# Moving the convolution statistics of a conformer/mLSTM block: none in the first head, the first mean product behind the second head's key projection

## The chip, the cores and the metric

The kernel runs on one core of one Trainium2 chip. The metric is the device time of one execution in microseconds (us); the time of a kernel is the median of several executions. A profile is taken of one execution more, and its times are counted from the start of its span. The engines are PE (TensorE, matrix products), DVE (VectorE), ACT (ScalarE), POOL (GpSimd) and SP, which here only issues DMAs. Each takes its own instructions in a fixed order that is set when the kernel is built; waits on semaphores tie the engines together.

## What is computed

One layer of a hybrid backbone over 512 latent tokens (a 1024-wide model) with 256 context tokens. Cut to the parts that matter here:

```
h  = adaLN(RMSNorm(x))                                  # latent and context tokens
p  = split(h @ w_in)                                    # GLU pair, q, k, v, output gate, scan gates, branch gates
u  = p[0] * sigmoid(p[1])                               # GLU, 1024 channels
u  = depthwise_conv(u, width 31, along rows of 64 tokens)
A  = silu(layernorm(u, over the 1024 channels)) @ w_conv_out     # branch A
B  = (norm(mLSTM(q, k, v)) * sigmoid(p[5])) @ w_m_out            # branch B, 4 heads, both directions
x += gate1 * ((sigmoid(p[7]) * A + sigmoid(p[8]) * B) @ w_out)
x += gate2 * squared_relu_mlp(adaLN(RMSNorm(x)))
out = RMSNorm(x)
```

The layer norm of branch A needs, for each token, the mean and the mean square over all 1024 channels.

## The kernel before, in words

All matrix products with weights are done in three passes: each operand is split into a high and a low half (`split`, `wpiece`), and `mm3` (lines 105 to 108) issues high x high, high x low and low x high. `mlast[0]` holds the last matmul that `mm3` issued. A weight piece of 512 KB is loaded by SP into `wraw` (three buffers), its high half made by ACT (line 100) and its low half by DVE (line 101), four buffers of each.

The stages run in this order: modulation and the six early branch-gate tiles; more gate tiles and the queries of head 0 (`q_proj`); the scan gates; the keys of head 0 (`k_proj`); then the loop over four heads (lines 653 to 665); then the tail with branch A's and B's output products and the MLP.

For heads 1 to 3 the loop runs `k_proj(h)`, in heads 1 and 3 one `glu_tile`, `q_proj(h)` and `attend`; `attend` also does the two steps of another GLU tile among the scores (heads 0 to 2), and a further `glu_tile` follows it (heads 0 to 2). So the eight GLU tiles of 128 channels are spread as two in head 0, three in head 1, two in head 2 and one in head 3.

`attend` computes the head's output gate (`p5`), for four query tiles of 128 tokens the scores (`spc`, `spl`) and the weights `pm_`, transposes those on PE (`tp`), then the six value tiles (`pv`, 144 matmuls), and then the output of the four query tiles (`po`). The value tiles take two PSUM banks of the one tag and four of the other; the tag "b" has four banks and serves `tp`, the GLU products `pg`, the queries `pq`, four of the value tiles, `po`, and the mean product `pm0`.

A GLU tile ends in `conv31`: 31 taps on a tile of 128 channels x 512 tokens. The first is ACT's (line 431), the other 30 are DVE's (line 433), one instruction each, into an accumulator `ca` (two buffers) from the padded input `up` (two buffers). The taps are given a priority lowered by 800, so that the scheduler, which fixes the order of each engine's instructions before the run, uses them to fill in among others. `conv31` then puts one portion, `lnstat(j, ...)`, into the list `queue`; `pump(n)` takes up to n portions from that list and issues them where it is called.

`lnstat` (lines 443 to 456) is what the change moves. For tile 0 it first makes a rough mean per token: a product of the matrix of ones with the convolved tile into `pm0` (line 446; an fp32 product, which the trace shows as two matmuls on a tile it calls `pm`), and ACT's copy of it into `lnm0` (line 447). Every tile then has this mean subtracted (DVE, line 448) and is stored to DRAM (SP, line 449); its sum and its squares are collected in two running tiles, by ACT for tile 0 (lines 451, 452) and by ACT and DVE for the others (454 to 456). `lnfinish` (lines 458 to 469) turns the two into the mean and the reciprocal deviation in the last head.

Before the change `pump(9)` is called in every head at two places in `attend`: ahead of the value projection (line 586) and behind the outputs (line 630). In the last head `lnend` calls it once more ahead of `lnfinish`. Since the list is never longer than nine, each call empties it. The calls ahead of the value projection therefore issue tile 0 in head 0; tiles 1, 2 and 3 in head 1; tiles 4 and 5 in head 2; tiles 6 and 7 in head 3; the calls behind the outputs find nothing.

Of the kernel before, what the change touches and what calls it, by code (L numbers as in the profile page):

```python
# [47 lines left out]
def block(ctx, tc, a, out):  # L48
    nc = tc.nc
    mm = nc.tensor.matmul  # L50
# [11 lines left out]
    ones = cst.tile([P, P], F32, name="ones")  # L62
# [26 lines left out]
    mlast = [None]  # L89
# [51 lines left out]
    def pump(n):  # L141
        while n > 0 and queue:
            queue.popleft()()
            n -= 1

    with ExitStack() as hs:
# [9 lines left out]
        def bank(nm):  # L156
            return ps.tile([P, 512], F32, tag="b", name=nm, bufs=4)
# [211 lines left out]
        def qk_tile(h, i, which, hi, lo):  # L369
            f = (16 if which == "k" else 0) + 4 * h + i  # L370
            w = wpiece(a["wqk"][f], (KT, P))
            raw = hq2.tile([P, 774], F32, tag="craw", name="craw")
            acc = hq2.tile([P, 770], F32, tag="cacc", name="cacc")
            wc = O_QK + 5 * f
            if which == "k":
                pk, pl = bank_a("pk"), bank_a("pl")
                projT(pk, w, 0, C)
                projT(pl, w, C, T)
                for o in (0, 258, 772):
                    nc.gpsimd.memset(raw[:, o:o + 2], 0.0)  # L380
                nc.scalar.copy(out=raw[:, 2:258], in_=pk[:, 0:C])
                nc.scalar.copy(out=raw[:, 260:772], in_=pl)
                n, segs = 770, ((0, 0, C), (258, C, T))
            else:
                pk = bank("pq")
                projT(pk, w, C, T)
                for o in (0, 514):
                    nc.gpsimd.memset(raw[:, o:o + 2], 0.0)
                nc.scalar.copy(out=raw[:, 2:514], in_=pk)
                n, segs = 512, ((0, 0, T),)  # L390
            nc.scalar.activation(out=acc[:, :n], in_=raw[:, 0:n], func=AF.Copy, scale=ccol(wc))  # L391
            for d in range(1, 5):
                nc.vector.scalar_tensor_tensor(out=acc[:, :n], in0=raw[:, d:d + n], scalar=ccol(wc + d),  # L393
                                               in1=acc[:, :n], op0=ALU.mult, op1=ALU.add)
            tot = segs[-1][1] + segs[-1][2]
            for s, o, m in segs:
                nc.scalar.activation(out=raw[:, o:o + m], in_=acc[:, s:s + m], func=AF.Silu)
            split(hi[:, i, :], lo[:, i, :], raw[:, :tot])
            tick()

        def glu_steps(j):
            up = hq2.tile([P, 8, 94], F32, tag="up", name="up")
            u = up[:, :, 15:79]

            def step(s):
                w = wpiece(a["wglu"][s, j], (KT, P))
                pg = bank("pg")
                projT(pg, w, C, T)
                pv = pg.rearrange("p (r c) -> p r c", r=8)
                if s:  # L410
                    nc.gpsimd.memset(up[:, :, 0:15], 0.0)
                    nc.gpsimd.memset(up[:, :, 79:94], 0.0)
                    nc.scalar.activation(out=u, in_=pv, func=AF.Sigmoid)
                else:
                    nc.vector.tensor_tensor(out=u, in0=pv, in1=u, op=ALU.mult)
                    conv31(j, up)
                tick()
            return [lambda: step(1), lambda: step(0)]

        def glu_tile(j):  # L420
            for st in glu_steps(j):
                st()

        def conv31(j, up):
            acc = hqa.tile([P, T], F32, tag="ca", name="ca", bufs=2)
            accv = acc.rearrange("p (r c) -> p r c", r=8)

            def tap(d):
                w_ = ccol(O_DW + 31 * j + d)
                if d == 0:  # L430
                    nc.scalar.activation(out=accv, in_=up[:, :, 0:64], func=AF.Copy, scale=w_)
                else:
                    nc.vector.scalar_tensor_tensor(out=accv, in0=up[:, :, d:d + 64], scalar=w_, in1=accv,  # L433
                                                   op0=ALU.mult, op1=ALU.add)
            with tc.high_priority(offset=-LOWP):
                for d in range(31):
                    tap(d)
            queue.append(lambda: lnstat(j, acc, up.rearrange("p r c -> p (r c)")[:, :T]))
# [4 lines left out]
        def lnstat(j, acc, sq):  # L443
            if j == 0:
                pm0 = bank("pm0")
                mm(pm0, lhsT=ones, rhs=acc, start=True, stop=True)
                nc.scalar.activation(out=ln["m0"], in_=pm0, func=AF.Copy, scale=1.0 / P)
            nc.vector.tensor_tensor(out=acc, in0=acc, in1=ln["m0"], op=ALU.subtract)
            nc.sync.dma_start(out=cdr[j], in_=acc)
            if j == 0:  # L450
                nc.scalar.copy(out=ln["s1"], in_=acc)
                nc.scalar.activation(out=ln["s2"], in_=acc, func=AF.Square)
            else:
                nc.scalar.activation(out=sq, in_=acc, func=AF.Square)
                nc.vector.tensor_tensor(out=ln["s1"], in0=ln["s1"], in1=acc, op=ALU.add)
                nc.vector.tensor_tensor(out=ln["s2"], in0=ln["s2"], in1=sq, op=ALU.add)
# [14 lines left out]
        def ab_early(i):  # L471
            w = wpiece(a["wab"][i - NS], (KT, P))
            pg = bank("pab")
            projT(pg, w, C, T)
            so = hq2.tile([P, T], F32, tag="cacc", name="so")
            nc.scalar.activation(out=so, in_=pg, func=AF.Sigmoid)
            nc.sync.dma_start(out=sd[i], in_=so)
            tick()

        def k_proj(h):  # L480
            khi = pools["kv"].tile([P, 4, TOK], F32R, tag="kvh", name="khi")
            klo = pools["kv"].tile([P, 4, TOK], F32R, tag="kvl", name="klo")
            for i in range(4):
                qk_tile(h, i, "k", khi, klo)
            return khi, klo

        def q_proj(h):
            qhi = hq.tile([P, 4, T], F32R, tag="qh", name="qhi")
            qlo = hq.tile([P, 4, T], F32R, tag="ql", name="qlo")
            for i in range(4):  # L490
                qk_tile(h, i, "q", qhi, qlo)
            return qhi, qlo
# [14 lines left out]
        def attend(h, he, he2, khi, klo, qhi, qlo, more, mid):  # L507
# [15 lines left out]
            for t in range(NT):  # L523
# [59 lines left out]
                    js = slice(3 * hf, 3 * hf + 3)  # L583
                    split(pth[:, js, :], ptl[:, js, :], tp[:, :384].rearrange("p (j t) -> p j t", j=3))
                Ps.append((pth, ptl))
            pump(9)
            nc.scalar.activation(out=sg, in_=sg, func=AF.Sigmoid)
            vhi = pools["kv"].tile([P, 6, HD], F32R, tag="kvh", name="vhi")
            vlo = pools["kv"].tile([P, 6, HD], F32R, tag="kvl", name="vlo")
# [23 lines left out]
            for t in range(NT):  # L613
# [13 lines left out]
                pend = (t, hm)  # L627
                if mid and t == 1:
                    mid()
            pump(9)  # L630
            if h == H - 1:
                store(*pend)

# [19 lines left out]
        for h in range(H):  # L653
            if h:
                kh = k_proj(h)
                if h == 1 or h == H - 1:
                    glu_tile(next(glus))
                qh = q_proj(h)
            if h < H - 1:
                attend(h, he, he2, *kh, *qh, lambda: glu_steps(next(glus)), None)  # L660
            else:
                attend(h, he, he2, *kh, *qh,
                              lambda: [lambda i=i: ab_early(i) for i in range(NS + NX, NS + NX + NE)], lnend)
            if h < H - 1:
                glu_tile(next(glus))
# [403 lines left out]
def build(shapes):  # L1069
    import concourse.bacc as bacc  # L1070
    import concourse.tile as tile

    nc = bacc.Bacc("TRN2", target_bir_lowering=False, num_devices=1, dynamic_dma_scratch_size=4096)
    aps = {k: nc.dram_tensor(f"in_{k}", s, F32, kind="ExternalInput").ap() for k, s in shapes.items()}
    out = nc.dram_tensor("out_0_dram", (T, D), F32, kind="ExternalOutput").ap()
    with tile.TileContext(nc) as tc:
        block(tc, aps, out)
    return nc
# [10 lines left out]
```

## Time and profile before

| | us |
|---|---|
| median of 3 runs | 1362.58 |
| lowest and highest of them | 1361.43, 1363.29 |
| the profiled execution, its own time | 1359.83 |
| its span, from the first to the last instruction | 1358.1 |
| busy PE, weight loads of PE, DVE, ACT, POOL | 1316.8, 1096.3, 949.6, 591.3, 63.3 |
| mean granted clock of PE, share of full | 0.991 |

A row of a group or a timeline gives the line of the kernel, the engine and operation, the written tile `<-` the read tiles, and the shapes; "x18" is the number of instructions merged into the row. In square brackets stands the idle time of the engine ahead of it and what ended that. Matmuls are pipelined, so the step from one start to the next is their cost and not the duration shown. Heads are found in the trace by their tiles: head 0's value matmuls begin at 208.12 us, head 1's at 406.56, head 2's at 573.56, head 3's at 751.44.

### The profile page before, as it was taken

The numbers are of one execution on the slowest core, as the hardware profiler recorded it, in microseconds if no ns is written. First come the engines' busy times: TensorE is split into PE (matmuls) and PEld (weight loads), VectorE is DVE, ScalarE is ACT, GpSimd is POOL, SyncE is SP. The second block draws the span as 40 slices with busy tenths as digits, with TensorE's granted clock in tenths as the row PEclk, the third lists the DMA queues.
The fourth block names the chain that finished last, engine by engine and source line by source line (L and its number), as shares of the span: only waits on it lengthen the run. The fifth ranks groups of instructions, "written<-read, shape, count | busy, mean of one in ns | idle before, by whom it ended". The sixth has DMA issues, their size and how long they took to land. (4 is left out here: it accounts for less than half of the span.)

```text
span 1358.1 us, 16564 instructions
## 1 busy us (share of the span) xinstructions
PE 1316.8 (97%) x6214; PEld 1096.3 (81%) x6214; DVE 949.6 (70%) x1480; ACT 591.3 (44%) x857; POOL 63.3 (5%) x223
## 2 busy tenths in 40 slices
PE   6999995999999999999999999999999999999997
PEld 4778883888888888888888878888898888888886
DVE  6687868269989498695999358866576554555536
ACT  5548662226463255722555346322345323342224
POOL 1000100000010000000000010110010000000000
PEclk9999997999999999999999999999999999999999
DMA  9793331232332323323232458875634322333212
GB/s 368 281 328 112 104 115 49 77 71 74 105 124 70 78 63 115 103 70 78 76 103 90 155 164 292 286 226 161 226 110 146 103 78 78 124 109 94 68 40 78
DMA packets 84067, 176.35 MB, mean 130 GB/s; under 512 B 31729, under 2 KB 38033, under 8 KB 83986
## 3 DMA queue, kind: packets, MB, share of 16 engines
q1 hardware_dynamic: 78802, 157.46, 36.1%
q0 software_dynamic: 4608, 16.78, 3.9%
q8 instruction: 49, 0.80, 0.2%
q10 hardware_dynamic: 576, 1.05, 0.2%
q14 instruction: 32, 0.26, 0.1%
HBM read 163.25 MB, written 12.01 MB: 129 GB/s over the span
## 5 line engine op out<-in xcount | busy, mean ns | idle before, releaser
L100 ACT CAST whi<-wraw 128x1024 fp32r<-128x1024 f32 (+1 forms) x159 | 164.6, 1039 | 290.1 <-PE pv L108 70.5
L101 DVE TENSOR_TENSOR wlo<-wraw,whi 128x1024 fp32r<-128x1024 f32 (+1 forms) x159 | 191.7, 1207 | 86.6 <-ACT whi L100 85.7
L433 DVE SCALAR_TENSOR_TENSOR ca<-up,col,ca 128x512 f32<-128x512 f32 x240 | 179.6, 749 | 4.8
L393 DVE SCALAR_TENSOR_TENSOR cacc<-craw,col,cacc 128x512 f32<-128x512 f32 (+1 forms) x128 | 111.6, 879 | 2.4 <-ACT cacc L391 1.8
L107 PE MATMUL pf<-w2l,fT 128*128 128x512 f32 x256 | 99.6, 390 | 0.0
L108 PE MATMUL pf<-w2h,fT 128*128 128x512 f32 x256 | 99.5, 389 | 0.0
L955 ACT CAST w2h<-w2raw 128x1024 fp32r<-128x1024 f32 x32 | 32.3, 1053 | 154.3 <-PE pf L108 124.5
L106 PE MATMUL pf<-w2h,fT 128*128 128x512 f32 x256 | 99.3, 390 | 0.1
L975 DVE TENSOR_TENSOR x<-pf,x 128x512 f32<-128x512 f32 x64 | 44.1, 689 | 69.0 <-PE pf L108 68.9
L106 PE MATMUL pf<-h2T,whi 128*128 128x512 f32 x224 | 87.2, 389 | 0.0
L107 PE MATMUL pf<-h2T,whi 128*128 128x512 f32 x224 | 87.2, 389 | 0.0
L108 PE MATMUL pf<-h2T,wlo 128*128 128x512 f32 x224 | 87.1, 389 | 0.0
L106 PE MATMUL pv<-whi,hT 128*128 128x512 f32 x192 | 76.7, 400 | 0.0
L108 PE MATMUL pv<-whi,hT 128*128 128x512 f32 x192 | 75.5, 393 | 0.0
L107 PE MATMUL pv<-wlo,hT 128*128 128x512 f32 x192 | 75.4, 393 | 0.0
L953 DVE TENSOR_TENSOR w2raw<-w2raw,ga 128x1024 f32<-128x1024 f32 x32 | 39.0, 1224 | 43.2 <-DMA w2raw<-in_w 40.4
L107 PEld LDWEIGHTS pf<-w2l,fT 128*128 128x128 f32 x256 | 48.0, 188 | 10.6 <-DVE w2l L960 0.7
L106 PEld LDWEIGHTS pf<-w2h,fT 128*128 128x128 f32 x256 | 48.0, 188 | 10.5 <-ACT w2h L955 0.5
L108 PEld LDWEIGHTS pf<-w2h,fT 128*128 128x128 f32 x256 | 48.0, 188 | 9.9
L960 DVE TENSOR_TENSOR w2l<-w2raw,w2h 128x512 fp32r<-128x512 f32 x64 | 40.5, 685 | 15.6 <-ACT w2h L955 15.6
L106 PE MATMUL pq<-hT,whi 128*128 128x512 f32 x128 | 50.2, 392 | 0.0
L106 PE MATMUL pg<-hT,whi 128*128 128x512 f32 x128 | 50.1, 391 | 0.0
(362 smaller groups left out, 3316.0 us busy)
## 6 DMA issues: line engine op xcount, KB each, us to landing
wm<-in_wmt SPq DMA_DIRECT2D x32, 512.0 KB, 4.5
wmt<-in_wmt POOLq DMA_DIRECT2D x32, 512.0 KB, 4.8
wraw<-in_wqk SPq DMA_DIRECT2D x32, 512.0 KB, 3.5
wraw<-in_w SPq DMA_DIRECT2D x32, 512.0 KB, 4.6
w2raw<-in_w SPq DMA_DIRECT2D x32, 512.0 KB, 3.6
wraw<-in_wp SPq DMA_DIRECT2D x16, 512.0 KB, 3.6
wraw<-in_wglu SPq DMA_DIRECT2D x16, 512.0 KB, 3.6
wraw<-in_wv SPq DMA_DIRECT2D x16, 512.0 KB, 3.6
```

Of the source, the lines that this page charges most:

```text
L100: pin("act", lambda: nc.scalar.copy(out=hi[:, s], in_=raw[:, s]))
L101: wlast[0] = pin("dve", lambda: nc.vector.tensor_tensor(out=lo[:, s], in0=raw[:, s], in1=hi[:, s].bitcast(F32), op=ALU.subtract))
L106: mm(dst, lhsT=l[0], rhs=r[0], start=start, stop=False)
L107: mm(dst, lhsT=l[0], rhs=r[1], start=False, stop=False)
L108: mlast[0] = mm(dst, lhsT=l[1], rhs=r[0], start=False, stop=stop)
L393: nc.vector.scalar_tensor_tensor(out=acc[:, :n], in0=raw[:, d:d + n], scalar=ccol(wc + d), in1=acc[:, :n], op0=ALU.mult, op1=ALU.add)
L433: nc.vector.scalar_tensor_tensor(out=accv, in0=up[:, :, d:d + 64], scalar=w_, in1=accv, op0=ALU.mult, op1=ALU.add)
L953: nc.vector.tensor_tensor(out=raw, in0=raw, in1=ga2, op=ALU.mult)
L955: nc.scalar.copy(out=hi, in_=raw)
L960: nc.vector.tensor_tensor(out=l_, in0=raw[:, nn], in1=hi[:, nn].bitcast(F32), op=ALU.subtract)
L975: nc.vector.tensor_tensor(out=x1[t][:, nn], in0=pf, in1=x1[t][:, nn], op=ALU.add)
```

## The change

The mean product of tile 0 gets an order edge: it stands on PE behind the last `mm3` matmul issued when its portion is taken. Both calls of `pump` in `attend` take nothing in head 0. A third call is added in heads 1 to 3, right behind the key projection. So the portions of tiles 0 and 1 are issued behind the keys of head 1, ahead of the GLU tile that follows them; tiles 2 and 3 in the attention of head 1; tile 4 behind the keys of head 2, tile 5 in its attention; tile 6 behind the keys of head 3, tile 7 in its attention. The GLU tiles and convolutions themselves stay where they were in the program. No instruction is added or removed.

```diff
         def lnstat(j, acc, sq):
             if j == 0:
                 pm0 = bank("pm0")
-                mm(pm0, lhsT=ones, rhs=acc, start=True, stop=True)
+                with tc.issue_after(mlast[0].ins):
+                    mm(pm0, lhsT=ones, rhs=acc, start=True, stop=True)
                 nc.scalar.activation(out=ln["m0"], in_=pm0, func=AF.Copy, scale=1.0 / P)
...
                 Ps.append((pth, ptl))
-            pump(9)
+
+            pump(9 if h else 0)
             nc.scalar.activation(out=sg, in_=sg, func=AF.Sigmoid)
...
                 if mid and t == 1:
                     mid()
-            pump(9)
+            pump(9 if h else 0)
             if h == H - 1:
                 store(*pend)
...
         for h in range(H):
             if h:
                 kh = k_proj(h)
+                pump(9)
                 if h == 1 or h == H - 1:
                     glu_tile(next(glus))
                 qh = q_proj(h)
```

## The prediction

> **What bounds the kernel now.** I read the page first, then the list of who waited for whom on PE, then PE's and DVE's timelines around the longest of those waits, then tables by stretches that set one head beside another.
>
> ```profile
> PE 1316.8 (97%) x6214; PEld 1096.3 (81%) x6214; DVE 949.6 (70%) x1480; ACT 591.3 (44%) x857; POOL 63.3 (5%) x223
> PE   6999995999999999999999999999999999999997
> DVE  6687868269989498695999358866576554555536
> PEclk9999997999999999999999999999999999999999
> ```
>
> PE is busy 97% of the 1358.1 us span. Of its 40 slices only a few are not full, and the seventh (204 to 238 us) is both the emptiest and the one slice with a lower granted clock. The waits of PE say what happened there:
>
> ```profile
> PE pm L446 <- DVE ca L433: 16.6, 1, 16.6
> PE pt L237 <- DVE xt L204: 6.8, 2, 5.8
> PE th L600 <- DVE hm L621: 0.7, 1, 0.7
> PE spc L107 <- DVE klo L112: 0.6, 1, 0.6
> ```
>
> Columns: total us, times, longest. One matmul, the sum over channels of the first convolution tile (the trace calls its tile `pm`), waits 16.6 us for the last tap of that convolution. PE takes its instructions in order, so all PE work behind it waits too. PE's timeline at that place, and how long the same work takes in each head:
>
> ```profile
> 218.88 0.39 PE L108 MATMUL pv<-whi,hT 128*128 128x512 f32 x1
> 235.87 2.04 PE L446 MATMUL pm<-ca,ones 128*128 128x512 f32 x2 [16.60 <-DVE ca L433]
> 236.93 1.41 PE L106 MATMUL pv<-whi,hT 128*128 128x512 f32 x1
> 208.12:261.43 53.31, 36.71 (x150) 29.17 (x148) 32.15 (x43) 11.10 (x18) 0.63 (x3) 0.81 0.14 45
> 406.56:439.31 32.75, 32.75 (x148) 27.11 (x146) 31.20 (x43) 9.38 (x16) 0.29 (x1) 1.00 0.20 67
> 573.56:606.31 32.75, 32.75 (x148) 27.11 (x146) 30.65 (x42) 9.47 (x15) 0.29 (x1) 1.00 0.20 65
> ```
>
> The last three rows run from the first value-projection matmul of heads 0, 1 and 2 to the first output matmul (columns: length, then busy PE, PEld, DVE, ACT, POOL, granted clock, DMA share, GB/s). The same 144 value matmuls take 53.31 us in head 0 and 32.75 us in heads 1 and 2. Head 0 has the mean product inside that stretch; the others have none. Heads 1 and 2 also have their own convolution beside the stretch (DVE 31.20 and 30.65 us busy of 32.75) and PE loses nothing.
>
> **Part 1: the wait goes.** The change issues nothing of the queue in head 0 and puts the mean product behind head 1's last key matmul. What is left of head 0's stretch is what head 1 has: 53.31 - 32.75 = 20.56 us less. This is more than the 16.60 us of waiting, because the clock falls during the wait:
>
> ```profile
> 221.30:235.80 14.50, 0.00 (x0) 0.50 0.00 0
> 235.80:241.70 5.90, 5.83 (x12) 0.50 0.13 47
> 242.20:261.40 19.20, 19.20 (x86) 1.00 0.24 81
> ```
>
> The number behind PE's count is the granted clock: 0.50 while PE idles, still 0.50 for 5.90 us of work after it, then 1.00. Half of 5.90 is 2.95 us; 16.60 + 2.95 = 19.55, and the mean product itself makes up the rest of 20.56 (next part). The Trainium skill ("TensorE: Matmul & The Clock Gate", What's actually happening) puts the return to full clock at about 3.4 us of sustained work; by that the slow tail would cost 1.7 us and the saving would be 1.25 us smaller. The row's 5.90 us is used, since the 20.56 us contain it.
>
> **Part 2: the mean product in its new place.** It is 2 recorded matmuls of fp32 against the matrix of ones. Four of the same shape run near the end of the heads at full clock:
>
> ```profile
> 792.79 1.02 PE L461 MATMUL ps<-lns,ones 128*128 128x512 f32 x2
> 793.65 1.02 PE L462 MATMUL ps<-lns,ones 128*128 128x512 f32 x2
> 794.10 0.79 PE L106 MATMUL po<-vhi,pth 128*128 128x512 f32 x1
> 794.74 0.40 PE L107 MATMUL po<-vlo,pth 128*128 128x512 f32 x1
> 321.76 0.39 PE L108 MATMUL pl<-hT,wlo 128*128 128x512 f32 x1
> 321.99 0.39 PE L106 MATMUL pg<-hT,whi 128*128 128x512 f32 x1
> ```
>
> From the first of them to the second po matmul are 794.74 - 792.79 = 1.95 us, of which one po matmul is 0.23 (the step from 321.76 to 321.99 is such a step): 1.72 / 4 = 0.43 us each, so the product costs 0.86 us of PE. Nothing hides it, as PE is full on both sides of its new place, which is the step from 321.76 to 321.99 (head 1's last key matmul, first GLU matmul). It can wait there only if the first convolution is unfinished:
>
> ```profile
> 211.20 8.62 DVE L433 SCALAR_TENSOR_TENSOR ca<-up,col,ca 128x512 f32<-128x512 f32 x11
> 221.60 14.13 DVE L433 SCALAR_TENSOR_TENSOR ca<-up,col,ca 128x512 f32<-128x512 f32 x18
> 238.58 0.69 DVE L448 TENSOR_TENSOR ca<-ca,lnm 128x512 f32<-128x512 f32 x1 [2.86 <-ACT lnm L447]
> 236.00:284.00 48.00, 14.12 (x17) 0.94 0.29 71
> 284.00:340.00 56.00, 51.70 (x63) 1.00 0.25 76
> 340.00:389.00 49.00, 48.61 (x91) 1.00 0.31 98
> ```
>
> The last three rows are DVE alone. Eleven taps are done before PE stalls; the 18 that today run inside the stall (14.13 us) find 48.00 - 14.12 = 33.88 us of free DVE between 236 and 284, which on the new clock is the time just behind the value projection. So the convolution ends about when it does today (221.60 + 14.13 = 235.7), and the product comes at about 322 - 20.56 = 301; no wait: 0. If that cover were gone, the price is in the third rival.
>
> **Part 3: what follows the product.** The same portion holds the copy of the mean (ACT), the subtraction L448 (DVE), a copy and a square (ACT) and the store L449 through SP. Today these run behind the stall; afterwards they run from about 322 on (old time), where DVE has 4.30 us free of 56.00 (284 to 340) and then 0.39 of 49.00 (340 to 389). DVE takes instructions in order, so the subtraction, and any wait of it for ACT's copy of the mean, delays everything queued behind it there: key and query splits, weight halves, head 1's scores. Who waits for that is PE's transpose of the second query tile:
>
> ```profile
> 388.74 0.34 DVE L568 TENSOR_SCALAR pm__3187<-E,dn 128x256 f32<-128x256 f32 x1
> 389.59 0.82 PE L582 MATMUL tp<-ident,pm__3187 128*128 128x128 f32 x6
> SPq L449 <- DVE ca L448: 44.0, 8, 28.5
> ```
>
> The tile is ready at 389.08 and used at 389.59: 0.51 us of slack. So the cost has these ends: below nothing, the 0.6 us of spc and the 0.7 us of th from the waits could go if the order shifts kindly (-1.3); above, the subtraction and as long a wait for ACT as today's, 0.69 + 2.86 - 0.51 = 3.04. I take 0.69 - 0.51 = 0.18, as the wait of 2.86 came from a mean product at half clock with nothing else for DVE to do. [...]
>
> On SP the store is moved past the loads of head 0's value weights and head 1's key weights. Today it holds the queue up to 28.5 us (the row above), which ends with the stall; behind k's loads it holds head 1's later weight loads for as long as the subtraction is late, a few us at most, covered by three weight buffers of 24 matmuls each (24 x 0.23 = 5.5 us a piece): 0. POOL's fills of the padding wait for the same tiles as before, 0.
>
> **Part 4: the other portions.** Tile 1's goes with tile 0's; tiles 4 and 6 move from the attention to behind the key projection of heads 2 and 3. Each begins when its own convolution ends, wherever it is written:
>
> ```profile
> 337.70 1.41 DVE L433 SCALAR_TENSOR_TENSOR ca<-up,col,ca 128x512 f32<-128x512 f32 x2
> 339.02 0.69 DVE L448 TENSOR_TENSOR ca<-ca,lnm 128x512 f32<-128x512 f32 x1
> ```
>
> Tile 1's subtraction follows its last tap by nothing already. An earlier place in the program can't advance that, and the number of instructions is the same: 0, with an end on either side inside those of part 3.
>
> **The sum.** The profiled execution took 1359.83 us (span 1358.1, and 1.73 outside it): 1359.83 - 20.56 + 0.86 + 0.18 = 1340.31. The median of the runs shown, 1362.58, lies 2.75 above the profiled execution, so the median forecast is **1343.1 us**. Nothing gives the shift back later: behind the stall PE's only listed waits up to the end of the heads are the 0.7 of th, and loads are issued as buffers come free, so they shift along.
>
> **Rivals.** First, DVE late in head 1, or in head 0's stretch, where the low halves of v queue behind taps. For it: 0.39 us free DVE and 0.51 us slack. Against it: head 1 carries nearly the same DVE load in 32.75 us and its PE waits for nothing. Price 3.04 in place of 0.18: 1359.83 - 20.56 + 0.86 + 3.04 + 2.75 = 1345.9 us.
>
> Second, the change doesn't do what it says: the 96 value matmuls behind the stall wait for something else, such as sums that still hold their PSUM banks. Then only the name of the wait changes and the time stays 1362.6. Against it: heads 1 and 2 use the same banks in the same order and run all 144 in 32.75 us.
>
> Third, on the other side: the taps have low priority, and DVE's order is fixed before the run. If they are put behind head 1's key work, PE comes to the product first and stalls again, now with DVE sharing its time. The stall is decided by how many taps are left: a tap is 14.13 / 18 = 0.785 us, so beyond 16.60 / 0.785 = 21 of 30 taps it is slower than before. All 30 left would be 23.6 us of waiting, 7.0 over today's 16.60, with the same slow tail: 1362.6 + 7.0 = 1369.6 us. Against it: 11 taps run before 219.8 already, and 33.88 us are free behind them.
>
> **How the numbers follow.** Forecast 0.80; first rival 0.14; second 0.03; third 0.03. A difference of 0.2%, 2.7 us, is about what a measurement of this kernel can tell from none. Forecast and first rival are faster by far more: 0.94; within it 0.03; slower 0.03. The range holds the first two cases with their bounds: below, 1343.1 - 0.18 - 1.3 = 1341.6; above, 1345.9; and 2.0 us at each end, as the executions shown spread from 1359.83 to 1363.29. That is 1339.6 to 1347.9.
>
> **What would show it.** Right: no wait of PE on the mean product; head 0's value stretch 32.75 us long at clock 1.00; the product behind head 1's key matmuls, 0.86 us; no new wait over 1 us on PE. Wrong: a wait before the transposes or output matmuls of heads 0 and 1 (first rival); value matmuls in head 0 still in two parts (second); the product waiting for taps at its new place (third).

## The result, and the profile after

The changed kernel takes 1342.66 us (median of 4 runs, 1341.42 to 1342.93) against 1362.37 us before (4 runs): a ratio of 0.9854, 95% interval 0.9837 to 0.9871, so 19.7 us faster. The prediction said 1343.1, 0.4 us more.

The page of the changed kernel: busy times, the slices of PE and its clock.

```profile
PE 1314.7 (98%) x6214; PEld 1095.2 (82%) x6214; DVE 949.5 (71%) x1480; ACT 591.1 (44%) x857; POOL 64.0 (5%) x223
PE   6999999999999999999999999999999999999997
PEclk9999999999999999999999999999999999999999
```

The hole in the seventh slice and the one low digit of the clock are gone, at the same number of instructions on every engine. The list of PE's waits no longer has the mean product; what leads it now lies in the start-up:

```profile
PE pt L237 <- DVE xt L204: 7.3, 2, 6.3
PE sacc L106 <- ACT hT L242: 2.9, 2, 2.6
PE pcr L169 <- DMA cL<-in_c: 2.4, 1, 2.4
```

Tables by stretches (length; then busy PE, PEld, DVE, ACT, POOL with counts; granted clock; DMA share; GB/s). First the kernel after: head 0's value stretch, then from head 0's first value matmul to head 1's, then from head 1's to head 2's.

```profile
209.62:242.37 32.75, 32.75 (x147) 27.12 (x146) 30.96 (x42) 9.35 (x15) 0.63 (x3) 1.00 0.21 66
209.62:388.42 178.80, 178.80 (x870) 150.70 (x868) 154.30 (x248) 83.96 (x123) 9.03 (x42) 1.00 0.30 88
388.42:555.42 167.00, 167.00 (x820) 141.32 (x818) 130.29 (x214) 76.40 (x113) 8.44 (x40) 1.00 0.31 88
```

The last two stretches in the kernel before:

```profile
208.12:406.56 198.44, 181.84 (x870) 152.37 (x868) 154.45 (x248) 83.87 (x123) 9.16 (x42) 0.95 0.27 80
406.56:573.56 167.00, 167.00 (x820) 141.29 (x818) 130.29 (x214) 76.07 (x113) 7.47 (x40) 1.00 0.31 88
```

Head 0's value stretch is 32.75 us, to the hundredth what heads 1 and 2 had. From head 0 to head 1 the kernel saves 198.44 - 178.80 = 19.64 us, and from head 1 to head 2 the two agree: 167.00 us each. Since such stretches repeat so closely, they are the measure below. Whole times do not repeat so well: head 0's value stretch began at 208.12 us in the profiled execution of before and at 209.62 in that of after, 1.50 us apart ahead of anything that was moved (over all thirteen profiles of this study from 208.12 to 212.64). That is most of why the two profiled executions differ by only 1359.83 - 1341.42 = 18.41 us while the medians differ by 19.7.

PE at the product's new place, in the kernel after:

```profile
302.71 0.40 PE L108 MATMUL pl<-hT,wlo 128*128 128x512 f32 x1
302.94 1.02 PE L447 MATMUL pm<-ca,ones 128*128 128x512 f32 x2
303.40 0.80 PE L106 MATMUL pg<-hT,whi 128*128 128x512 f32 x1
304.04 0.40 PE L107 MATMUL pg<-hT,whi 128*128 128x512 f32 x1
```

It waits for nothing, and from its start to the second GLU matmul it takes 304.04 - 302.94 = 1.10 us, 0.87 more than one GLU step of 0.23. The last tap is long done (DVE, kernel after):

```profile
239.67 0.74 DVE L433 SCALAR_TENSOR_TENSOR ca<-up,col,ca 128x512 f32<-128x512 f32 x1
240.33 1.28 DVE L112 TENSOR_TENSOR vlo<-pv,vhi 128x512 fp32r<-128x512 f32 x2
```

The tap ends at 240.41, 62.5 us ahead of the product.

### The profile page after: what moved, and what is told of

Same layout as the page of the kernel before. It is cut to its first block, busy times and chain, and to the rows that moved or that the text cites. A ratio compares the mean times of both kernels' runs of the same rounds, so it can differ in the third digit from the quotient of the medians.

```text
span 1339.7 us, 16566 instructions
## 1 busy us (share of the span) xinstructions
PE 1314.7 (98%) x6214; PEld 1095.2 (82%) x6214; DVE 949.5 (71%) x1480; ACT 591.1 (44%) x857; POOL 64.0 (5%) x223
```

## The experiments

The theory on trial: PE works in order, so the product's place in that order decides; a wait there costs itself plus a tail at half clock; anywhere behind the last tap the product costs only its own 0.86 us. The rivals on trial: the order edge, the PSUM bank, or the other moved portions carry the gain; or DVE's full stretch in head 1 takes some of it back.

**One part alone: the edge.** Before, with

```diff
-                mm(pm0, lhsT=ones, rhs=acc, start=True, stop=True)
+                with tc.issue_after(mlast[0].ins):
+                    mm(pm0, lhsT=ones, rhs=acc, start=True, stop=True)
```

> Only the order edge is added; the portions are taken where they were. Theory: the place of the product on PE is what counts, and the last three-pass matmul issued when the portion of tile 0 is taken is one of head 0's GLU tile, which stands ahead of the value projection anyway; so the product stays behind the 48th value matmul, PE waits 16.6 us again, 1362.4 us as before. Rival: the edge alone brings the gain, 1342.7 us.

Measured: 1361.62 us, ratio 0.9993 (0.9984 to 1.0003). PE waits as before:

```profile
PE pm L447 <- DVE ca L433: 16.5, 1, 16.5
```

**The other part alone: the moved portions.** After, with the edge taken out again.

> All three places where portions are taken are as after the change; the order edge is left out. Theory: by the order that is fixed before the run the product comes behind the last key matmul of head 1 without the edge too, so 1342.7 us, within 2 us of the kernel after. Rival: without the edge the product comes too early again and PE waits, 1350 to 1362 us.

Measured: 1341.75 us, ratio 0.9845 (0.983 to 0.9859). From head 0 to head 1 it takes what the full change takes:

```profile
209.78:388.58 178.80, 178.80 (x870) 150.71 (x868) 154.13 (x248) 83.94 (x123) 8.77 (x42) 1.00 0.30 89
```

So the edge changes nothing in this kernel; taking the portion later does all of it.

**Another PSUM bank.** Before, with `pm0 = bank_a("pm0")` in place of `bank("pm0")`.

> The kernel before, with the mean product in a PSUM bank of the other tag, so that the last four value tiles need not queue behind it. The order then puts it behind the 96th value matmul in place of the 48th: 208.1 + 96 x 0.229 = 230.1 us, with the taps done at 236 to 239. Theory (PE is in order, a wait costs itself and a tail of about 3 us at half clock): a wait of 6 to 9 us and 1342.7 + 9 to 12 = 1351.7 to 1354.7 us. Rival (the bank was the whole cause, PE passes over the product): 1342.7 us. Second rival (a wait of this size costs no clock): 1348.7 to 1351.7 us.

Measured: 1352.26 us, ratio 0.9919 (0.9905 to 0.9934). The product stands behind the 96th value matmul and waits:

```profile
PE pm L446 <- DVE ca L433: 6.5, 1, 6.5
```

So the bank has a part in where the product stood: with another it comes 48 matmuls later. That this is so because the old tag is shared with four of the six value tiles is argued, not shown. PE still waits at the product, so the bank was not the whole cause.

**A third place.** Before, with one edit: the call ahead of the value projection takes nothing in head 0, so that the call behind the outputs finds the portion.

```diff
-            pump(9)
+            pump(9 if h else 0)
             nc.scalar.activation(out=sg, in_=sg, func=AF.Sigmoid)
```

> The kernel before with one edit: head 0 takes no portion ahead of its value projection; the second call of head 0, behind its outputs, takes it. The product then stands behind the 72 output matmuls of head 0, some 16 us after the last tap. Theory: any place behind the last tap is as good as the one of the change; no wait on the product, 1342.7 us within 2 us, and the tiles 1, 4 and 6 taken late cost nothing. Rival (the place behind the keys, or the earlier portions of tiles 4 and 6, carry part of the gain): 1345 us or more.

Measured: 1341.98 us, ratio 0.9843 (0.9827 to 0.986). PE, and the stretch from head 0 to head 1:

```profile
260.44 0.40 PE L108 MATMUL po<-vhi,ptl 128*128 128x512 f32 x1
260.68 1.02 PE L446 MATMUL pm<-ca,ones 128*128 128x512 f32 x2
```

```profile
211.60:390.39 178.79, 178.79 (x869) 150.68 (x868) 153.80 (x248) 83.86 (x123) 8.64 (x42) 1.00 0.30 89
```

A one-line edit gives the whole gain, 178.79 against 178.80 us. The third call behind the keys, and with it the earlier portions of tiles 1, 4 and 6, is worth nothing that the trace shows: from head 1 to head 2 and from head 2 to head 3 this kernel takes 167.00 and 177.88 us, and so does the change.

**Shorter waits.** The kernel before, with fewer taps for the first channel tile, so that its last tap comes earlier: `range(31 if j else 16)`, `range(31 if j else 23)` and `range(31 if j else 9)` in `conv31`. Less of the convolution is computed in these three.

> The kernel before, with 15 of the 31 taps of the first channel tile left out (the convolution of that tile is cut to width 16); the product still stands behind the 48th value matmul. Theory (PE waits for the last tap, and a wait costs itself and the half-clock tail): 15 taps of 0.75 to 0.785 us are 11.3 to 11.8 us less waiting, so a wait of about 5 us is left, with a tail of 1 to 3 us, in all 1342.7 + 5 + 1 to 3 = 1348.7 to 1350.7 us. Rival (the wait is for something else than the taps): 1362.4 us. Second rival (a wait this short leaves the clock at 1.00): 1347.7 us.

> The kernel before with 8 of the 31 taps of the first channel tile left out. Theory: a wait of 16.6 - 8 x 0.785 = 10.3 us behind the 48th value matmul, and a tail at half clock between the 2.40 us found behind a wait of 6.5 and the 3.0 to 3.1 behind 16.5, so head 0's value stretch takes 32.75 + 0.86 + 10.3 + 2.7 = 46.6 us. Rival (the tail is one fixed cost): 3.0 us in any case, 46.9 us.

> The kernel before with 22 of the 31 taps of the first channel tile left out; the product then stands behind the 39th value matmul. Theory: the last tap ends about 10 us after the first value matmul, the 39 take 8.9, so a wait of 1 us, too short for the clock to fall: head 0's value stretch 32.75 + 0.86 + 1 = 34.6 us at clock 1.00. Rival (each wait of PE costs a tail): 36 us or more, with a clock below 1.

Measured: 1350.47 us with 15 taps less (ratio 0.9915, 0.9892 to 0.9937); in one execution each, 1355.74 with 8 less and 1343.68 with 22 less. Head 0's value stretch in five kernels, one row of each trace: the edge alone (31 taps), 8 less, the other bank, 15 less, 22 less.

```profile
210.07:263.20 53.13, 36.61 (x150) 29.12 (x149) 32.16 (x43) 11.02 (x17) 1.69 (x3) 0.84 0.14 45
```

```profile
210.97:257.61 46.64, 36.20 (x150) 28.80 (x148) 26.15 (x35) 11.25 (x18) 0.63 (x3) 0.89 0.15 52
```

```profile
211.08:253.61 42.53, 36.01 (x149) 28.43 (x148) 31.51 (x43) 11.29 (x18) 0.63 (x3) 0.92 0.14 43
```

```profile
209.95:250.29 40.34, 35.53 (x149) 28.28 (x147) 21.01 (x28) 10.98 (x17) 0.63 (x3) 0.96 0.18 59
```

```profile
211.07:245.29 34.22, 33.86 (x149) 27.42 (x148) 15.89 (x21) 11.00 (x18) 0.63 (x3) 1.00 0.20 70
```

The length less busy PE is the wait: 16.52, 10.44, 6.52, 4.81 and 0.36 us. It follows the taps. Busy PE less 32.75 and less 0.92 for the product (next run) is what PE loses beyond the wait, the tail: 2.94, 2.53, 2.34, 1.86 and 0.19 us. With 22 taps less the clock stays at 1.00, so a wait of 0.36 us cost no clock there, and the 0.19 has another cause. The other four, and the kernel before, have a stretch at half clock. Here it is for before (a wait of 16.60), the edge alone, 8 less, the other bank and 15 less, one row of each trace (length, then busy PE, granted clock, DMA share, GB/s):

```profile
221.35:241.80 20.45, 5.93 (x12) 0.50 0.04 14
226.40:243.40 17.00, 5.66 (x11) 0.50 0.04 16
227.20:237.40 10.20, 4.84 (x10) 0.50 0.07 23
237.00:243.78 6.78, 3.90 (x7) 0.50 0.00 0
226.10:229.48 3.38, 3.38 (x7) 0.50 0.02 5
```

Half of the busy PE in these rows, 2.97, 2.83, 2.42, 1.95 and 1.69 us, is most of the tail. Up to the moments at which the clock changes, the stretches last 20.48, 17.07, 10.24, 6.83 and 3.41 us, that is six, five, three, two and one times 3.41. They begin between 2.1 and 5.2 us after PE's last matmul ahead of the wait; with 15 taps less that is 0.18 us after the wait has ended, so all 3.41 us fall on work. So in these executions the tail is not one fixed size, and a wait of 4.81 us did not leave the clock alone. But how a tail depends on the length of its wait is not shown: the nearly equal waits of the first two rows have slow stretches of six and of five steps, so it also matters where the steps happen to lie, and there is one traced execution of each kernel. Executions of one kernel differ as well: the four with 15 taps less have mean granted clocks from 0.995 to 0.998 and take from 1349.28 to 1353.19 us.

**Without the product.** After, without the rough mean:

```diff
-            if j == 0:
-                pm0 = bank("pm0")
-                with tc.issue_after(mlast[0].ins):
-                    mm(pm0, lhsT=ones, rhs=acc, start=True, stop=True)
-                nc.scalar.activation(out=ln["m0"], in_=pm0, func=AF.Copy, scale=1.0 / P)
-            nc.vector.tensor_tensor(out=acc, in0=acc, in1=ln["m0"], op=ALU.subtract)
```

> The kernel after without the rough mean: its product, ACT's copy and the eight subtractions are left out, so the sums are taken of the convolved values themselves; the norm that follows subtracts the mean in any case, so that only the rounding differs. Theory: nothing hides the product at its new place, so 0.86 us less, 1342.7 - 0.86 = 1341.8 us, and the stretch from head 0's to head 1's first value matmul falls from 178.79 to 177.9 us. Rival (the product fits into a step that PE has to spare, or the subtractions cost PE time): 178.79 again, or less than 177.5 us.

Measured: 1341.07 us, ratio 0.9845 (0.9828 to 0.9862), an interval that overlaps the change's own. The stretch tells more:

```profile
212.64:390.52 177.88, 177.88 (x867) 150.32 (x866) 152.07 (x245) 83.15 (x122) 7.62 (x42) 1.00 0.30 89
```

178.80 - 177.88 = 0.92 us is the product's share of PE's path. The subtractions left out with it add nothing that shows: from head 1 to head 2, where they alone are left out, it is 167.00 us with and without them. ACT's copy was not left out by itself. By this stretch it is the fastest version of the study, by 0.9 us over the change; the run times alone can't tell them apart. What it gives up is the centring of the values ahead of their sums.

**More work for DVE.** After, with more passes of DVE over tile 0 behind its subtraction, and with the first tile's taps issued twice, which makes its convolution another one.

```diff
             nc.vector.tensor_tensor(out=acc, in0=acc, in1=ln["m0"], op=ALU.subtract)
+            for _ in range(6 if j == 0 else 0):
+                nc.vector.tensor_scalar(out=acc, in0=acc, scalar1=1.0, scalar2=None, op0=ALU.mult)
```

> The kernel after, with six more passes of DVE over tile 0 (multiply by one, 128x512) right behind its subtraction, 6 x 0.43 = 2.6 us at most, in the stretch of head 1 where DVE is full and the prediction put 0.51 us of slack. Theory of the prediction: beyond the slack it is one for one, 1342.7 + 2 = 1344.7 us. Rival, which the trace of the kernel after favours (its slack at the same transpose is 0.58 us although DVE got the subtraction): the taps of low priority give way, no loss, 1342.7 us.

> As the run with six, with twelve more passes, 5.1 us at most. Theory of the prediction: 1342.7 + 4.6 = 1347.3 us. Rival (taps give way): 1342.7 us, with tile 2's last tap some 5 us later and nobody waiting for it.

```diff
                 for d in range(31):
                     tap(d)
+                for d in range(1, 31 if j == 0 else 1):
+                    tap(d)
```

> The kernel after, with the 30 DVE taps of the first channel tile issued twice (30 more instructions, so another convolution for that tile), 22.5 us more of DVE. Theory: the product stands some 60 us behind the last tap and DVE is free for some 34 us there, so nothing waits, 1342.7 us within 2 us. Rival (the cover is thin, or DVE's full stretch in head 1 takes the surplus): the product waits or head 1's splits come late, 1350 us or more.

Measured: 1343.45 us (0.9861, 0.9842 to 0.988), 1343.48 (0.9859, 0.9836 to 0.9881) and 1343.34 (0.986, 0.9841 to 0.988). None is clear of the change, but the stretches are. First twelve passes, from head 1 to head 2, and the wait of PE that is new there; then doubled taps, from head 0 to head 1 and from head 1 to head 2, and the two waits that are new:

```profile
390.12:557.88 167.76, 167.42 (x819) 141.14 (x818) 130.95 (x215) 78.16 (x115) 9.14 (x43) 1.00 0.31 89
```

```profile
PE po L107 <- DVE vlo L112: 0.3, 1, 0.3
```

```profile
211.24:390.46 179.22, 179.03 (x870) 150.61 (x868) 172.18 (x277) 82.88 (x121) 9.76 (x43) 1.00 0.30 86
390.46:558.24 167.78, 167.40 (x819) 141.15 (x818) 131.64 (x215) 78.51 (x115) 8.53 (x40) 1.00 0.31 90
```

```profile
PE tp L585 <- DVE pm__3222 L568: 0.2, 1, 0.2
PE po L106 <- DVE vlo L112: 0.4, 1, 0.4
```

Against 178.80 and 167.00, twelve passes cost 0.76 us and 30 more taps 0.42 + 0.78 = 1.20 us. Six passes already cost 0.60 (from head 1 to head 2 it takes 167.60), so the loss does not follow the number of passes. By the pages of the profiles DVE was busy 3.5 us longer than in the change with twelve passes and 20.3 us longer with the taps; one for one beyond the slack of 0.51 would have been some 3 and 20. Both theories were off in part: the taps give way almost wholly, but not wholly. That it is the taps that give way shows in the 70 us from the product's start on, in the change and with twelve passes (DVE's taps alone: length, busy, clock, DMA share, GB/s):

```profile
302.94:372.94 70.00, 28.95 (x39) 1.00 0.31 99
304.64:374.64 70.00, 25.49 (x34) 1.00 0.32 99
```

Five taps less are done there, while DVE is as busy as before, 69.41 us against 69.55. Where a loss appears it is where the first rival put it: at the transposes and at the output matmuls that want the low halves of v.

## Why the prediction was right, point by point

- **Part 1, the wait (20.56 us).** Right in place and size: head 0's stretch is 32.75 us at clock 1.00. To read the saving from the other heads, and not from the 16.6 us in the list of waits, was what got the clock's share in. The short-wait runs confirm that there is a tail of the wait. Its split is a little off: the 1.01 us that it leaves for the product between 19.55 and 20.56 is 0.92 for the product, and the other 0.09 may be of the kind seen behind the wait of 0.36 us, where the clock had no part. The Trainium skill's return to full clock after about 3.4 us of work ("TensorE: Matmul & The Clock Gate", What's actually happening) was taken in the prediction as the whole time of slow work; by that the saving would have been an estimated 1.25 us smaller. The section gives it as the least: full clock comes after at least one busy window of about 3.4 us, and the windows run free of the kernel. The traces agree with that, with 3.4 to 5.9 us of slow work and slow stretches of whole multiples of 3.41.
- **Part 2, the product (0.86 us).** 0.92 us by the run without it, 0.87 by the timeline; on PE's path, as said. The cover holds: 30 more taps don't make the product wait.
- **Part 3, DVE (0.18 us).** The one term that failed, by its whole small size. 198.44 - 20.56 + 0.92 = 178.80 is what is measured, so it was 0.00. The step that failed is 0.69 - 0.51, which lets the subtraction delay the transpose by all that it takes beyond the slack: DVE's 0.39 us of free time was no measure of its spare time. Much of what filled it were taps of low priority (in the last row below, 31 of the 99 instructions and 22.38 of the 51.69 us), and these can be done later. In the kernel after, the same transpose still has 0.59 us of slack in place of 0.51, though DVE is as full as before (its timeline, PE's, and the table of DVE alone):

```profile
369.08 0.47 DVE L566 SCALAR_TENSOR_TENSOR pm__3192<-E,dn,pm__3192 128x256 f32<-128x256 f32 x1
370.52 0.34 DVE L566 SCALAR_TENSOR_TENSOR pm__3192<-E,dn,pm__3192 128x128 f32<-128x128 f32 x1
```

```profile
371.45 0.82 PE L583 MATMUL tp<-ident,pm__3192 128*128 128x128 f32 x6
```

```profile
320.00:372.00 52.00, 51.69 (x99) 1.00 0.33 105
```

  The tile is ready at 370.86 and used at 371.45; DVE has 0.31 us free of 52.00 there. The Trainium skill ("Perfetto Trace Analysis", Identifying the Most-Contended Engine) takes the engine of highest occupancy as the one to relieve first, and judges PE by its rate of operations and its weight loads instead. With weight loads busy for 43.84 of these 52.00 us, that would make DVE the bound, and the whole 0.69 would have counted. The trace disagrees: the subtraction cost nothing, and 12 passes of some 0.43 us each cost 0.76 in all.
- **Part 4, the other portions (0).** Right: the version that leaves them late takes 178.79, 167.00 and 177.88 us from head to head, the change 178.80, 167.00 and 177.88.
- **The whole.** By the parts 20.56 - 0.86 - 0.18 = 19.52 us were to be saved, and 19.64 were: 0.18 too much for DVE and 0.06 too little for the product. That the forecast of the median came within 0.4 us is partly luck, since it was reached by adding 2.75 us to one execution, and the start-up alone moved by up to 4.52 us between profiles.
- **The rivals.** The first did not happen in the change; its mechanism is real and was brought about with more DVE work, at 0.60 to 1.20 us in place of its 3.04. The second is out, since the value matmuls run as one block. The third did not happen. A wait longer than today's was not tried, so its price stays argued; that a wait costs itself and up to about 3 us was measured for waits from 0.36 to 16.6 us.

What stays open is why the order puts the product where the taps are unfinished. The order is fixed before the run, so it must count on the taps ending sooner than they do; that is argued, not shown.

## What to carry to other kernels

In this kernel the wait for a sum was gone once the sum stood behind other work that was ready; what was left was the sum's own 0.92 us. So first look for where its input is really done and then for a call site behind that; between the two sites tried, one behind the outputs and one behind the next keys, there was 0.01 us. Take the saving from a stretch elsewhere in the trace that does the same work without the wait, since it holds the clock's share as well. On an engine that is kept full by low-priority filling, free time need not measure spare time, as DVE showed here: add work and see.

## What the runs showed that was not expected

The tail at half clock is no fixed fee: 1.86 us of extra PE time behind a wait of 4.81, 2.34 behind 6.52, 2.53 behind 10.44, 2.94 behind 16.52, one execution each, and no loss of clock behind a wait of 0.36. The half clock comes in steps of 3.41 us and can begin when the wait is already over. And a stretch of this kernel repeats to 0.01 us from one version to another that does the same (178.80, 178.80 and 178.79 from head 0 to head 1), while the start-up ahead of it moved by up to 4.52 us between profiles (208.12 to 212.64): so small terms were better read from a stretch than from the run times.
